# Down as a block product in seven products for all token pairs, with the sums of h made in gate and up

## The chip, the cores and the metric

The kernel runs on one core of a Trainium2 chip. A core has TensorE (matmuls, PE in the profile, its weight loads PEld), VectorE (DVE), ScalarE (ACT), GpSimd (POOL) and SyncE (SP), which here only issues transfers, and 16 DMA engines. The metric is the device time of one execution in microseconds (us); lower is better. Times of the kernel before: 2737.86 us, the median of three runs (2736.7 to 2738.58).

## What is computed

Two layers of an encoder with a width of 1024, for 1024 prompt tokens and 64 sample tokens, with the same weights. Each layer is a mixer (retention in layer 0, differential attention in layer 1, beside a memory attention), a product with w_o, a norm, the feed-forward part, and a norm. Cut to what the change touches:

```python
def _swiglu(x, w_gate, w_up, w_down):
    return (jax.nn.silu(x @ w_gate) * (x @ w_up)) @ w_down
...
        xp = _post_norm(xp, _swiglu(xp, w_gate[i], w_up[i], w_down[i]), ln2_g[i], ln2_b[i])
...
        xs = _post_norm(xs, _swiglu(xs, w_gate[i], w_up[i], w_down[i]), ln2_g[i], ln2_b[i])
```

`_post_norm(x, y, g, b)` is the layer norm of ALPHA * x + y. The inner width is 2816: 22 blocks of 128. h is the product of silu and up, and "down" is h @ w_down, 1088 x 2816 by 2816 x 1024.

## The kernel before

**Arithmetic.** Everything is fp32. A matmul takes operands that are split in a high and a low part (fp32r), and a product is three matmuls: high by high, high by low, low by high. The sample has its 64 high and 64 low rows in one operand of 128, so it needs two. Prompt tokens are eight tiles of 128 (0 to 7); tile 8 is the sample.

**Weights.** The class Weights plans all weights of the program in one list. A unit is loaded raw by SP's queue, split by ACT (high, L231) and by VectorE (low, L244; for units of 384 columns POOL), and put into a ring of 8192 words, eight slots of 128 x 512 pairs. It runs ahead of the matmuls: `mm` (L294) calls `pump` behind every matmul, and the plan spends a count of TensorE time on when a raw is loaded, a high and a low are made. Raws lie in two buffers of tag "raw" and in t4 buffers.

**Gate and up** (`gate_up`, L1109) is a block product in seven products (P1 to P7) over pairs of token tiles already. For each of the 22 blocks of the inner width, weights of w_gate and w_up come in sums that POOL makes (`combine` L411 to L413, `combine4` L416), and seven products of two groups of columns (288 and 256) follow each other. At the end of P3 and P4 VectorE makes h of a block, and SP's queue stores it to `hd[l, ff]` in DRAM (L1180, L1188). Its operands, the split transposed X, lie in XT.

**Down** (`down`, L1240) goes through the tiles in three groups, DOWN = ((8, 0, 1), (2, 3, 4), (5, 6, 7)). For each group, it streams w_down (22 blocks of 128 x 1024) and the columns of h (`load_h` L1228 to L1233), in steps of two blocks. ACT and VectorE split h (L323, L326). A tile's two halves of 512 columns accumulate over all 22 blocks in PSUM (tags S, pj and A, two buffers each). At a group's end `finish` (L1273) adds ALPHA * X, and the norm follows (bn_stats L576, the reciprocal root L568 on POOL, apply L590 and L591). In layer 0 the tile is then transposed on TensorE into XT for the next mixer (`to_xt`, `tr` L299), as one of the pending pieces that down and the mixer take up; in layer 1 it is stored as the output. X comes from `mid` in DRAM by POOL's queue (L1221), a group at a time.

**Order.** Each engine runs its instructions in the order in which the program issues them. A queue's transfers are issued in that order too, and one that waits for its buffer or its data holds those behind it.

## Time and profile before

| what | value |
|---|---|
| median of three runs | 2737.86 us |
| the profiled execution's own time | 2741.43 us |
| its span | 2739.6 us, granted clock 0.98 |
| TensorE busy | 2639.4 us (96%), 16394 matmuls |
| VectorE, ACT, POOL busy | 1635.5 (60%), 1119.2 (41%), 503.6 us (18%) |
| DMA | 278.91 MB, 102 GB/s on the mean |
| of that w_down | 132 loads of 512 KB, both layers |
| chain that ended last | PE 85%, DVE 8%, ACT 2%, DMA 2% |

The profile comes from one execution with the hardware profiler on. Its span is what the trace's clock runs over; the rest of its time, 1.8 us, lies around it. Busy times are shares of the whole span and a mean over stages with different limits, so that a stage is read from its own stretch. The chain that ended last goes back from the last instruction, at each step to what released it. A wait of one engine costs time only where this chain goes through it.

### The profile page before, as it was taken

The page shows a single profiled execution, that of the slowest core. Times are in us where ns is not written, and L with a number is a line of the kernel's source. Part 1 is how long each engine was busy: PE and PEld are TensorE (multiplying, and loading weights), DVE is VectorE, ACT ScalarE, POOL GpSimd, SP SyncE. Part 2 cuts the span into 40 slices and gives each one's busy share as a digit, 9 for nine tenths or more (in the row PEclk, how much of TensorE's full clock was granted, in tenths as well). Part 3 has the DMA queues.
Part 4 walks back from the last instruction along what each step waited for, and adds up shares of the span by engine and source line. Part 5 has one row for each costly group of instructions (what it writes and reads, how often), then busy time and mean ns, then how long its engine had stood idle before and what let it go on. Part 6 is the DMA issues. An engine that isn't in the chain of part 4 may idle for free.

```text
span 2739.6 us, 44532 instructions
## 1 busy us (share of the span) xinstructions
PE 2639.4 (96%) x16394; PEld 2378.4 (87%) x16394; DVE 1635.5 (60%) x3799; ACT 1119.2 (41%) x2690; POOL 503.6 (18%) x529
## 2 busy tenths in 40 slices
PE   8999999989999999999999999999899999999997
PEld 7988887779999999877899999987699999998776
DVE  5766667784444444556567777777854444445664
ACT  5522223243333333434355555663343333334332
POOL 0022222132222230011111111101232222210110
PEclk9999999999999999999999999999899999999999
DMA  7121111432222224655311111123322222247662
GB/s 234 43 59 50 51 51 62 142 122 74 77 71 76 83 79 152 215 200 171 128 57 48 49 46 45 45 74 123 127 73 85 73 78 71 77 138 225 213 207 78
DMA packets 296090, 278.91 MB, mean 102 GB/s; under 512 B 63104, under 2 KB 257152, under 8 KB 295872
## 3 DMA queue, kind: packets, MB, share of 16 engines
q1 hardware_dynamic: 289424, 252.74, 29.7%
q0 software_dynamic: 6448, 23.33, 2.4%
q8 instruction: 129, 2.11, 0.3%
q14 instruction: 89, 0.73, 0.1%
HBM read 224.36 MB, written 51.64 MB: 101 GB/s over the span
## 4 chain that ended last, share of the span: by engine, by line
PE 85%; DVE 8%; ACT 2%; DMA 2%; issue 1%; POOL 1%; SPq 0%; DVEq 0%; POOLq 0%; ACTq 0%
PE pspj L294 39%; PE psS L294 23%; PE psA L294 19%; PE psA L299 3%; ACT de L919 1%; DVE dmx L913 1%; DVE ring L244 1%; DVE st L576 1%; DVE X L1273 1%; PE psS L299 1%; POOL rstd L568 0%; ACT ring L231 0%; DVE XT L326 0%; DVE T L326 0%; DVE X L591 0%
## 5 line engine op out<-in xcount | busy, mean ns | idle before, releaser
L294 PE MATMUL pspj<-ring,XT 128*128 128x512 f32 (+2 forms) x3024 | 680.8, 369 | 11.2 <-DVE ring L244 7.5
L244 DVE TENSOR_TENSOR ring<-raw,ring 128x512 fp32r<-128x512 f32 x558 | 384.2, 702 | 428.8 <-ACT ring L231 428.1
L231 ACT ACTIVATE ring<-raw 128x512 fp32r<-128x512 f32 (+1 forms) x606 | 367.3, 620 | 590.3 <-PE pspj L294 382.6
L294 PEld LDWEIGHTS pspj<-ring,XT 128*128 128x128 f32 x3024 | 526.5, 192 | 72.8 <-DVE ring L244 10.2
L294 PE MATMUL psS<-ring,hT 128*128 128x512 f32 x1496 | 361.3, 395 | 10.8 <-ACT hT L323 7.7
L294 PEld LDWEIGHTS psS<-ring,hT 128*128 128x128 f32 x1496 | 276.8, 188 | 83.6 <-ACT hT L323 16.5
L294 PE MATMUL psA<-XT,ring 128*128 128x288 f32 x2112 | 316.4, 296 | 0.0
L294 PEld LDWEIGHTS psA<-XT,ring 128*128 128x128 f32 x2112 | 291.5, 189 | 0.0
L294 PE MATMUL pspj<-XT,ring 128*128 128x256 f32 (+1 forms) x2112 | 281.2, 282 | 1.0 <-DVE XT L326 1.0
L294 PEld LDWEIGHTS pspj<-XT,ring 128*128 128x128 f32 x2112 | 266.3, 190 | 1.6 <-DVE XT L326 1.4
L294 PE MATMUL psS<-T,ring 128*128 128x288 f32 (+1 forms) x1890 | 262.0, 290 | 1.1 <-DVE s L1185 1.1
L294 PEld LDWEIGHTS psS<-T,ring 128*128 128x128 f32 x1890 | 244.4, 189 | 6.4 <-DVE s L1185 1.6
L244 DVE TENSOR_TENSOR ring<-sum,ring 128x512 fp32r<-128x512 f32 x132 | 98.3, 745 | 180.8 <-ACT ring L231 180.7
L416 POOL TENSOR_TENSOR sum<-raw,sum 128x512 f32<-128x512 f32 x44 | 56.9, 1293 | 635.4 <-DVE ring L244 619.6
L568 POOL TENSOR_TENSOR rstd<-mv,mhalf 128x1 f32<-128x1 f32 (+1 forms) x36 | 67.5, 1874 | 533.6 <-DVE mv L579 533.6
L231 ACT ACTIVATE ring<-sum 128x512 fp32r<-128x512 f32 x132 | 83.4, 632 | 143.3 <-PE psS L294 83.7
L294 PE MATMUL pspj<-wx,XT 128*128 128x512 f32 x432 | 113.3, 399 | 0.0
L294 PE MATMUL psA<-T,ring 128*128 128x288 f32 x570 | 89.6, 309 | 17.3 <-ACT ring L231 13.7
L294 PE MATMUL pspj<-ring,hT 128*128 128x512 f32 x396 | 103.6, 389 | 0.0
L294 PE MATMUL psA<-ring,hT 128*128 128x512 f32 x396 | 102.3, 390 | 0.2
L919 ACT ACTIVATE de<-psS,dmx 128x512 f32<-128x512 f32 (+4 forms) x156 | 88.6, 584 | 28.7 <-DVE dmx L916 28.7
L294 PEld LDWEIGHTS psA<-T,ring 128*128 128x128 f32 x570 | 82.7, 200 | 19.1 <-ACT ring L231 15.2
(239 smaller groups left out, 3849.1 us busy)
## 6 DMA issues: line engine op xcount, KB each, us to landing
raw<-in_w_down_dram SPq DMA_DIRECT2D x132, 512.0 KB, 4.2
raw<-in_w_gate_dram SPq DMA_DIRECT2D x44, 512.0 KB, 3.7
raw<-in_w_up_dram SPq DMA_DIRECT2D x44, 512.0 KB, 4.0
hr<-hd SPq DMA_DIRECT2D x88, 192.0 KB, 4.2
raw<-in_w_o_dram SPq DMA_DIRECT2D x32, 512.0 KB, 3.5
hd<-s SPq DMA_DIRECT2D x88, 144.0 KB, 2.0
raw<-in_ret_w_in_dram SPq DMA_DIRECT2D x48, 256.0 KB, 3.6
hd<-s SPq DMA_DIRECT2D x88, 128.0 KB, 3.4
```

The source lines that it names most:

```text
L231: k.nc.scalar.activation(s[:, 0], src(), AF.Copy)
L244: e.tensor_tensor(s[:, 1], src(), s[:, 0].bitcast(F32), op=OP.subtract)
L294: self.nc.tensor.matmul(out, l, r, start=start, stop=stop, skip_group_check=chain)
L299: self.nc.tensor.transpose(out, in_, ident)
L416: self.nc.gpsimd.tensor_tensor(sums[ff][1], part(ff, 0, 1), sums[ff][1], op=OP.subtract)
L568: self.nc.gpsimd.tensor_tensor(r[:n], var, self.mhalf[:n], op=OP.pow)
L576: nc.vector.bn_stats(st[:n, e], X[:n, e * 512:(e + 1) * 512])
L913: nc.vector.reduce_max(mx[:n, 2 * j:2 * j + 2], sp[:n, :, :m], axis=AX.X)
L919: nc.scalar.activation(e[:n, c, 512 * j:512 * j + m], sp[:n, c, :m], AF.Exp, bias=mx[:n, 4 + c:5 + c], scale=0.125, accum_out=mx[:n, 6 + 2 ...
L1273: nc.vector.scalar_tensor_tensor(X[t][:n, cs], X[t][:n, cs], ALPHA, dp[e][:n], op0=OP.mult, op1=OP.add)
```

## The change

Down becomes a block product as gate and up is one. The 22 blocks of the inner width are taken as 11 pairs, the output's 1024 columns as two halves, and the tokens as four pairs of tiles, PAIRS = ((0, 2), (1, 3), (4, 6), (5, 7)). So each block product is two by two by two, and is done in seven products of sums of blocks instead of eight (order 1, 7, 6, 5, 4, 3, 2). A product goes over 11 f for all four token pairs at once, each pair in a PSUM bank of its own, and its result is added into X on VectorE (`take`), by the table TAKES. The products 1, 6 and 5 share banks. The sample keeps its eight blocks without sums: it uses the single blocks of w_down beside products 1, 5, 3 and 2.

The sums of h are made in gate and up: POOL makes one sum behind each even block and three behind each odd one (`operands`), in two stages at the ring's end. The ring of gate and up is shorter by that, seven slots. The seven operands of an f, 128 x 512 each, are stored to `ho[l, p, f]`, the sample's split rows to `hs`. In down, SP loads them back one by one and ACT and VectorE split them.

The sums of w_down are made in down, on POOL (`plan_down`, L581, L588, L599, L611), in a room that XT's memory becomes while down runs; XT is two tiles now for that reason. Blocks of w_down are loaded into this room by SP's queue, either to a place of their own ("own", L541) or by one of six spare buffers of two blocks (L223). The low parts of products 3 and 2 are made on POOL. The last five f of product 2 are done pair by pair. The norm of the second tiles (2, 3, 6, 7) stands in product 3, that of the sample and the first tiles at the end, and layer 1's mixer takes its memory items in that order. All X loads stand in product 1.

The diff, cut:

```diff
-DOWN = ((8, 0, 1), (2, 3, 4), (5, 6, 7))
+PAIRS = ((0, 2), (1, 3), (4, 6), (5, 7))
+FIRSTS = tuple(a for a, _ in PAIRS)
+SECONDS = tuple(b for _, b in PAIRS)
+ORDER = (1, 7, 6, 5, 4, 3, 2)
+NF = NFF // 2
+TAKES = {7: ((1, 0, True), (1, 1, True)), 1: ((0, 0, True),), 6: ((1, 0, False),),
+         5: ((0, 1, True), (1, 1, False)), 4: ((1, 0, False),), 3: ((0, 1, False),), 2: ((0, 0, False),)}
+TAIL = 5
...
+RING_GATE_UP = 7168
+SPARE = 6
...
+        if self.raws[j][1] == "spare" and not self.k.xt_free:
+            return False
+        if self.raws[j][1] == "own":
+            return self.k.xt_free and self.next_split >= self.late[j] - 4
...
-        e = self.k.nc.gpsimd if cols == 384 else self.k.nc.vector
...
+            W.ptr, W.limit = 0, RING_GATE_UP
             self.plan_gate_up(l)
+            W.ptr, W.limit = 0, RING_WORDS
+            self.plan_down(l)
...
+    def plan_down(self, l):
+        W = self.W
+        w = self.i["w_down"][l]
+        tt = self.nc.gpsimd.tensor_tensor
+        def block(f, odd, half):
+            return w[(2 * f + odd) * 128:(2 * f + odd + 1) * 128, half * 512:(half + 1) * 512]
+        def load(v, src):
+            return (lambda raw: raw[:, v, :], src)
+        def own(f):
+            return W.add_into(lambda: self.nc.sync.dma_start(self.b11(f), block(f, 0, 0)))
+        def pairs(odd, half):
+            out = {}
+            for f in range(0, NF, 2):
+                out[f] = [load(v, block(f + v, odd, half)) for v in range(min(2, NF - f))]
+            return out
+        def unit(p, f, raws, src, before=None, **kw):
+            u = self.u_d[l, p, f] = W.add_unit(512, raws, src, **kw)
+            if before:
+                W.before_split[u] = before
+            if p in (3, 2):
+                W.low_on_pool.add(u)
+            if p != 1 or f >= 4:
+                W.wait_xt.add(u)
+            return u
+        held = {}
+        todo = pairs(0, 0)
+        for f in range(NF):
+            if f < 4:
+                if f % 2 == 0:
+                    held[f] = W.add_raw(todo[f])
+                j = held[f - f % 2]
+                unit(1, f, [j], lambda j=j, f=f: W.raw[j][:, f % 2, :])
+            else:
+                held[f] = own(f)
+                unit(1, f, [held[f]], lambda f=f: self.b11(f))
+        for f in range(NF):
+            if f < 4:
+                held["own", f] = own(f)
+            j = W.add_raw([load(0, block(f, 0, 1)), load(1, block(f, 1, 1))], "spare")
+            def t3(j=j, f=f):
+                c = self.chain(f)
+                raw = W.raw[j]
+                tt(c, raw[:, 1], raw[:, 0], op=OP.subtract)
+                W.released.add(j)
+            unit(7, f, [j], lambda f=f: self.chain(f), t3)
+        for f in range(NF):
+            unit(6, f, [held["own", f] if f < 4 else held[f]], lambda f=f: self.chain(f),
+                 lambda f=f: tt(self.chain(f), self.chain(f), self.b11(f), op=OP.add))
+        todo = pairs(0, 1)
+        for f in range(NF):
+            if f % 2 == 0:
+                j = W.add_raw(todo[f], "spare")
+            def part(j=j, f=f):
+                return W.raw[j][:, f % 2, :]
+            unit(5, f, [j], lambda f=f: self.b11(f),
+                 lambda f=f, part=part: tt(self.b11(f), part(), self.b11(f), op=OP.subtract))
+            unit(0, f, [j], part)
+        todo = pairs(1, 0)
+        for f in range(NF):
+            if f % 2 == 0:
+                j = W.add_raw(todo[f], "spare")
+            def part(j=j, f=f):
+                return W.raw[j][:, f % 2, :]
+            unit(4, f, [j], lambda f=f: self.chain(f),
+                 lambda f=f, part=part: tt(self.chain(f), part(), self.chain(f), op=OP.subtract))
+        for p, odd, half in ((3, 1, 1), (2, 1, 0)):
+            todo = pairs(odd, half)
+            for f in range(NF):
+                if f % 2 == 0:
+                    j = W.add_raw(todo[f])
+                unit(p, f, [j], lambda j=j, f=f: W.raw[j][:, f % 2, :])
...
-            nc.sync.dma_start(self.hd[l, ff][:, c:c + w[g]], a)
         def P4(ff, g, last=True):
             product(ff, 4, g, False, last)
             a, b = tile(ff, "s1", g), tile(ff, "s2", g)
             nc.vector.tensor_tensor(b, s[ff, "c3", g][:, :w[g]], b, op=OP.add)
             nc.vector.tensor_tensor(a, a, b, op=OP.mult)
+            if last:
+                operands(ff)
+        later = deque()
+        def store(dst, src):
+            later.append([6, dst, src])
+        def flush(all=False):
+            for x in later:
+                x[0] -= 1
+            while later and (all or later[0][0] <= 0):
+                _, dst, src = later.popleft()
+                (nc.gpsimd if dst.dtype == F32R else nc.sync).dma_start(dst, src)
+        def stage(i):
+            return self.ring_end[:, 512 * i:512 * (i + 1)]
+        def operands(ff):
+            f, odd = ff // 2, ff % 2
+            a, b = s[ff, "s1"], s[ff, "s4"]
+            hs = self.sm([128, 128], "hn", 3, F32R)
...
+            a, b = a[:, 32:544], b[:, 32:544]
+            store(self.hs[l, odd, f // 4][:, f % 4, :], hs)
+            tt = nc.gpsimd.tensor_tensor
+            if not odd:
+                store(self.ho[l, 1, f], a)
+                tt(stage(0), a, b, op=OP.subtract)
+                store(self.ho[l, 7, f], stage(0))
+                return
+            a0, b0 = s[ff - 1, "s1"][:, 32:544], s[ff - 1, "s4"][:, 32:544]
+            tt(stage(1), b0, b, op=OP.add)
+            tt(b0, stage(1), a0, op=OP.subtract)
+            tt(a0, a, b0, op=OP.subtract)
+            for p, x in ((6, b0), (5, stage(1)), (4, b), (3, a0), (2, a)):
+                store(self.ho[l, p, f], x)
...
+            if ff == 1:
+                both = both[1:3] + both[:1] + both[3:]
...
+        for i in range(2):
+            self.load_h(l, i)
+        self.load_sample(l, 0, 0)
+    def load_h(self, l, i):
+        p, f = ORDER[i // NF], i % NF
+        raw = self.hraw[i] = self.s2([128, 512], name="hr")
+        self.nc.sync.dma_start(raw, self.ho[l, p, f])
...
+    def split_op(self, i):
+        raw = self.hraw.pop(i)
+        if i < 2:
+            x = self.t4([128, 2, 512], F32R, "hT")
+            if i == 0:
+                self.keep = x
+        else:
+            c = (i - 2) % 5
+            x = self.keep if c == 4 else self.hslots[c // 2][:, c % 2]
+        self.hop[i] = x
+        self.split_h(x[:, 0], raw)
+        self.split_l(x[:, 1], raw, x[:, 0])
...
+        self.room = [self.xtp.tile([128, NF + SPARE, 512], F32, name=f"room{e}_{self.cnt}", tag="xt", bufs=2) for e in range(2)]
+        self.xt_free = True
+        self.hslots = [self.h9([128, 2, 2, 512], F32R, "hT") for _ in range(2)]
...
+        def load_x(t):
+            X[t] = self.t4([128, D], name=f"X{t}")
+            nc.gpsimd.dma_start(X[t][:self.ncol(t)], self.mid[l, t])
...
+        def take(t, half, ps, first):
+            x = X[t][:, half * 512:(half + 1) * 512]
+            if first:
+                nc.vector.scalar_tensor_tensor(x, x, ALPHA, ps, op0=OP.mult, op1=OP.add)
+            else:
+                nc.vector.tensor_tensor(x, ps, x, op=OP.add)
...
+        def product(p, f, pair, out, start, stop):
+            s = W.get(self.u_d[l, p, f])
+            wh, wl = s[:, 0], s[:, 1]
+            h = self.hop[ORDER.index(p) * NF + f]
+            c = slice(128 * pair, 128 * pair + 128)
+            self.mm(out, h[:, 0, c], wh, start, False, 512, chain=True)
+            self.mm(out, h[:, 0, c], wl, False, False, 512, chain=True)
+            self.mm(out, h[:, 1, c], wh, False, stop, 512, chain=True)
...
+        for j, t in enumerate(FIRSTS + (8,) + SECONDS):
+            chore(1, 1 + j, lambda t=t: load_x(t))
...
+        for j, t in enumerate(SECONDS):
+            chore(3, 1 + 2 * j, lambda t=t: norm(t))
+        def banks(kind):
+            if kind == "S":
+                out = [self.ps([128, 2, 512], "S") for _ in range(2)]
+                return [out[0][:, 0], out[0][:, 1], out[1][:, 0], out[1][:, 1]]
+            return [self.ps([128, 512], t) for t in ("pj", "pj", "A", "A")]
+        V = None
+        ahead(0, 3, 2)
+        for k, p in enumerate(ORDER):
+            if p == 1:
+                V = banks("V")
+            dps = V if p in (1, 6, 5) else banks("S")
...
+            def end(pair):
+                for which, e, fresh in TAKES[p]:
+                    take(PAIRS[pair][which], e, dps[pair], fresh)
+            whole = NF if p != 2 else NF - TAIL
+            for f in range(whole):
+                i = k * NF + f
+                for fn in chores.get((p, f), ()):
+                    fn()
+                for pair in range(4):
+                    product(p, f, pair, dps[pair], f == 0 and p not in (6, 5), f == NF - 1 and p not in (1, 6))
+                    if f == NF - 1:
+                        end(pair)
+                    if pair == 1:
+                        ahead(i, 6, 3)
+                    elif pair == 3 and self.pending and p in (3, 2):
                         self.pending.popleft()()
...
+        ahead(7 * NF, 7 * NF, 7 * NF)
+        for f in range(whole, NF):
+            sample(f, odd, self.u_d[l, unit, f], sp)
+        take_sample(half, sp, first)
+        norm(8)
+        for pair in range(4):
+            for f in range(whole, NF):
+                product(2, f, pair, dps[pair], False, f == NF - 1)
+                if pair == 3:
+                    W.done(self.u_d[l, 2, f])
+            end(pair)
+            norm(FIRSTS[pair], FIRSTS[3])
+            if self.pending:
+                self.pending.popleft()()
+        self.xt_free = False
```

What stands on TensorE's queue early in down of layer 1. psS, pspj and psA are the PSUM tiles by tag, ring holds weights, hT split h of one block (before) or of one f of a product (after). Before:

```order
L294 MATMUL psS_25322<-ring,hT_25306 128x512 x3
L294 MATMUL pspj_25348<-ring,hT_25301 128x512 x2
L294 MATMUL pspj_25348<-ring,hT_25306 128x512 x3
L294 MATMUL psA_25349<-ring,hT_25301 128x512 x3
L294 MATMUL psA_25349<-ring,hT_25306 128x512 x3
```

After, one f of product 1 (hs is the sample's operand):

```order
L356 MATMUL pspj_25531<-ring,hT_25521 128x512 x3
L356 MATMUL pspj_25532<-ring,hT_25521 128x512 x3
L356 MATMUL psA_25533<-ring,hT_25521 128x512 x3
L356 MATMUL psA_25534<-ring,hT_25521 128x512 x3
L356 MATMUL psS_25535<-ring,hs_25221 128x512 x2
```

Before, a tile's two halves are finished for two blocks, six matmuls a bank, before the next tile; now a row of the block product has one weight for each of four banks, and the sample's two matmuls stand behind each f.

SP's queue some way into the same down, from where h of block 8 is loaded. hr is raw h, raw a raw weight. Before:

```order
L1228 DMA hr_25494<-hd_8_174 128x256
L1229 DMA hr_25494<-hd_8_174 128x32
L1230 DMA hr_25494<-hd_8_174 128x32
L1228 DMA hr_25498<-hd_9_175 128x256
L1229 DMA hr_25498<-hd_9_175 128x32
L1230 DMA hr_25498<-hd_9_175 128x32
L1228 DMA hr_25556<-hd_10_176 128x256
L186 DMA raw_25457<-in_w_down_dram 128x1024
```

After (room is XT's memory; L541 loads a block to its own place, L223 a spare pair, L1459 an operand):

```order
L223 DMA room_3066_25519<-in_w_down_dram 128x512 x2
L1459 DMA hr_25609<-ho_1_7_230 128x512
L541 DMA room_3066_25520<-in_w_down_dram 128x512
L223 DMA room_3066_25519<-in_w_down_dram 128x512 x2
L541 DMA room_3066_25520<-in_w_down_dram 128x512
L223 DMA room_3066_25519<-in_w_down_dram 128x512 x2
L223 DMA room_3066_25520<-in_w_down_dram 128x512 x6
L1459 DMA hr_25648<-ho_1_8_231 128x512
L223 DMA room_3066_25519<-in_w_down_dram 128x512 x2
L1459 DMA hr_25674<-ho_1_9_232 128x512
```

Before, every few loads of h there is one or two of w_down; after, five spare pairs and two single blocks stand between the operands of f = 7 and f = 8.

POOL's queue at the passage from gate and up to down in layer 1. Before, from the last block's sums (L1221 loads X):

```order
L413 TENSOR_TENSOR raw_24647<-raw_24612,raw_24647 128x512
L416 TENSOR_TENSOR sum_24766<-raw_24612,sum_24766 128x512
L1221 DMA X_3092_25287<-mid_8_143 64x1024
L1221 DMA X_3093_25289<-mid_0_135 128x1024
L1221 DMA X_3094_25291<-mid_1_136 128x1024
L1221 DMA X_3113_25434<-mid_2_137 128x1024
L1221 DMA X_3114_25436<-mid_3_138 128x1024
L1221 DMA X_3115_25438<-mid_4_139 128x1024
```

After (L1498 loads X, L1410 to L1416 are the sums of h, L1390 and L1464 the sample's store and load, L581 and L588 sums of w_down):

```order
L1498 DMA X_3089_25684<-mid_8_145 64x1024
L1498 DMA X_3091_25709<-mid_2_139 128x1024
L1414 TENSOR_TENSOR ring_20340<-s_3049_25200,s_3062_25429 128x512
L1498 DMA X_3094_25736<-mid_3_140 128x1024
L1415 TENSOR_TENSOR s_3049_25200<-ring_20340,s_3039_24998 128x512
L1390 DMA hs_1_2_311<-hn_25504 128x128
L1416 TENSOR_TENSOR s_3039_24998<-s_3054_25238,s_3049_25200 128x512
L1498 DMA X_3096_25761<-mid_6_143 128x1024
L1498 DMA X_3098_25786<-mid_7_144 128x1024
L1464 DMA hs_25593<-hs_0_1_307 128x512
L581 TENSOR_TENSOR room_3066_25519<-room_3066_25520 128x512
```

The nine X loads stand between the last sums of h now, all ahead of the first sum of w_down; before, six stood at the start and three further on, behind norms.

## Rows read from the trace of the kernel before

**Rows 1.** Table of stretches: PE, PEld, DVE, ACT, POOL busy; PEclk, DMA share, GB/s

```profile
598.00:1079.30 481.30, 471.00 (x3673) 467.14 (x3673) 216.88 (x393) 182.94 (x391) 124.10 (x91) 0.98 0.27 83
...
2458.50:2725.50 267.00, 264.39 (x1146) 212.09 (x1144) 150.96 (x274) 105.12 (x211) 23.78 (x13) 1.00 0.57 188
```

**Rows 2.** Matmuls in order of time: start, us, line, out<-in, count [idle before <-releaser]

```profile
1079.33 0.63 PE L294 MATMUL psS<-ring,hT 128*128 128x512 f32 x2
...
1363.31 3.05 PE L294 MATMUL pspj<-ring,XT 128*128 128x256 f32 x24
...
2458.53 0.63 PE L294 MATMUL psS<-ring,hT 128*128 128x512 f32 x2
...
2723.94 1.52 PE L294 MATMUL psA<-ring,hT 128*128 128x512 f32 x6
```

**Rows 3.** Chain that ended last, in order of time: start, us, what

```profile
2709.14 5.44 PE psS L294 x24
```

**Rows 4.** Waits of TensorE in layer 0's, then layer 1's down: total, times, longest

```profile
PE psS L294 <- ACT hT L323: 6.9, 9, 2.0
...
PE psS L294 <- DVE hT L326: 1.7, 2, 1.2
```

**Rows 5.** Transposes on TensorE, and its waits, at the start of layer 1's mixer

```profile
1367.32 0.66 PE L299 MATMUL pspj<-ident,X 128*128 128x128 f32 x4 [0.96 <-DVE X L591]
1367.81 0.60 PE L299 MATMUL psA<-ident,X 128*128 128x128 f32 x4
...
PE pspj L294 <- ACT qdup L615: 3.5, 3, 1.5
PE pspj L299 <- DVE X L591: 1.0, 1, 1.0
```

**Rows 6.** Table of stretches again, two with saturated DMA

```profile
1080.00:1084.00 4.00, 4.00 (x18) 3.32 (x18) 1.83 (x6) 1.15 (x4) 0.00 (x0) 1.00 1.04 387
...
15.00:20.00 5.00, 5.00 (x23) 4.13 (x22) 3.94 (x6) 3.17 (x5) 0.00 (x0) 1.00 1.04 404
```

**Rows 7.** Groups of instructions in layer 1's down: count, busy us, mean ns

```profile
L244 DVE TENSOR_TENSOR ring<-raw,ring 128x512 fp32r<-128x512 f32 x125 | 83.6, 689 | 95.8 <-ACT ring L231 95.7
L326 DVE TENSOR_TENSOR hT<-hr,hT 128x384 fp32r<-128x384 f32 x44 | 24.0, 549 | 0.4
L1273 DVE SCALAR_TENSOR_TENSOR X<-X,psS 128x512 f32<-128x512 f32 x10 | 6.6, 676 | 11.0 <-PE psS L294 11.0
...
L231 ACT ACTIVATE ring<-raw 128x512 fp32r<-128x512 f32 x125 | 76.7, 626 | 122.3 <-PE pspj L294 120.5
L323 ACT ACTIVATE hT<-hr 128x384 fp32r<-128x384 f32 x44 | 22.5, 516 | 11.7 <-DVE ring L244 5.9 <-DMA out_dram<-X 5.4
...
L244 POOL TENSOR_TENSOR ring<-raw,ring 128x384 fp32r<-128x384 f32 x48 | 53.5, 1141 | 59.1 <-PE pspj L294 47.3 <-ACT ring L231 11.4 <-issue 0.2
```

**Rows 8.** Matmuls in order of time at the start of layer 0's gate and up

```profile
604.26 0.85 PE L294 MATMUL psA<-T,ring 128*128 128x288 f32 x2 [6.14 <-ACT ring L231]
605.95 5.64 PE L294 MATMUL psA<-T,ring 128*128 128x288 f32 x22 [0.83 <-ACT ring L231]
```

**Rows 9.** POOL's, then VectorE's instructions in order of time, in gate and up

```profile
705.66 1.62 POOL L412 TENSOR_TENSOR sum<-sum,raw 128x512 f32<-128x512 f32 x1
707.25 1.28 POOL L413 TENSOR_TENSOR raw<-raw,raw 128x512 f32<-128x512 f32 x1
...
702.26 0.69 DVE L244 TENSOR_TENSOR ring<-sum,ring 128x512 fp32r<-128x512 f32 x1 [0.20 <-ACT ring L231]
705.29 0.84 DVE L244 TENSOR_TENSOR ring<-raw,ring 128x512 fp32r<-128x512 f32 x1 [2.33 <-ACT ring L231]
```

**Rows 10.** VectorE's last instructions of the kernel, in order of time

```profile
2734.24 1.41 DVE L591 SCALAR_TENSOR_TENSOR X<-X,rstd,gb 128x512 f32<-128x512 f32 x2
```

**Rows 11.** Matmuls in order of time, one product of gate and up in layer 0

```profile
1069.46 1.76 PE L294 MATMUL psA<-XT,ring 128*128 128x288 f32 x12
...
1072.48 1.76 PE L294 MATMUL psA<-XT,ring 128*128 128x288 f32 x12
```

325 lines of the change are left out of this document (180 added, 145 removed).

## The prediction

> **What bounds the kernel now.** First the table of stretches: from 598 to 1079 us (gate and up of layer 0) TensorE is busy 471 of 481 us, and in layer 1's down 264 of 267, at a granted clock of 0.98 and 1.00 [rows 1]. DMA is at 27% and 57%, VectorE under 60%. Then the list of matmuls in order of time, for the edges of the two downs: 1079.33 to 1363.31 us, 284.0 us, in layer 0, and from 2458.53 us to the end of the last six matmuls at 2725.46, 266.9 us, in layer 1 [rows 2]. Last the chain that ended last, which runs through TensorE alone until 2722.8: 24 matmuls of 512 columns in 5.44 us, 226.7 ns each [rows 3]. A down has 22 steps of 52 matmuls (sixteen halves of prompt tiles with three each, two of the sample with two each), 1144, which at that pace take 259.3 us. So layer 1's down loses 7.6 us to waits, and layer 0's loses 24.7, of which the tables of waits name 6.9 for operands that the group change left unsplit [rows 4], and six tile transposes take some 1.1 us each (eight in 1.1 us [rows 5]). Down is bound by the count of matmuls. A change of its count is worth 0.227 us a matmul as long as everything that feeds it keeps up, and that is the question here.
>
> **The change, part by part.**
>
> *Matmuls.* Seven products of 11 blocks, four token pairs, three matmuls each are 924; the sample keeps 4 x 11 units of two, 88. 1012 against 1144: 132 fewer a layer. 1012 x 0.2267 = 229.4 us a layer.
>
> *First operands and banks.* Product 1 starts when the last gate-and-up results have left the four banks that it takes. I charge 1.5 us a layer, the longer waits of the earlier starts being 1.2 to 2.0 us [rows 4].
>
> *The burst ahead of product 1.* This is the term I trust least. Before, loads went out a few at a time. Now nine X tiles (4.5 MB, by POOL's queue), eleven blocks of 256 KB (2.9 MB) and, by the SP order, seven spare pairs of half a megabyte (3.7 MB) stand ahead of the operand of f = 8, with three operands and gate and up's last stores (2 MB): 13 MB. The blocks and spares go where XT lay, so none can start before gate and up's last products. On SP the stores hold everything behind them until the last sums are made on POOL, some 4.5 us into the down; by then I count some 3.5 MB gone, 9.5 to go. The nearest saturated stretches moved 387 and 404 GB/s [rows 6]; at 385 it is 24.7 us, so the operand lands at about 30 us. Its step starts at 8 x 14 x 0.2267 = 25.4, and the split needs 1.9 before it (516 ns ACT and 549 ns VectorE for 384 columns, both a third more for 512, and the queue of the step before [rows 7]): needed at 23.5. Late by some 7 us, and a further 1 for a clock that falls in the gap: where TensorE had been idle for 6.1 us, the next 24 matmuls of 288 columns took 7.3 us [rows 8], against 3.1 at the warm pace (24 x 0.2267 x 288/512). I take 8 us a layer, bounds 0 (X served late, or the pairs spread) and 11.
>  The Trainium skill ("DMA: Bandwidth & Descriptors", Specifications) gives about 358 GB/s as the limit of one core at HBM. The two saturated rows are above it; by it the burst would take 26.5 us and the stall be 2 us longer in each layer.
>
> *Feeding the steady part.* In products 7, 6 and 4 a block f lasts 12 x 0.2267 = 2.72 us, in 1, 5, 3 and 2 (with a sample unit) 3.17. ACT splits a weight and an operand: 0.63 + 0.62 = 1.25 us. VectorE makes two lows, 2 x 0.69 = 1.38. POOL makes one weight sum, 1.28 to 1.62 [rows 9]. In product 5 there is a sample unit to split as well: ACT 1.9, VectorE 2.1, of 3.17. The lows that move to POOL (products 3 and 2) are 1141 ns for 384 columns, so some 1.52 for 512. None reaches the step [rows 7], so I cost all of this at nothing; TensorE covers it, and the margin is thin only where VectorE and POOL share. DMA over a whole down falls: 81 blocks of 256 KB instead of 66 of 512 KB, while operands rise from 12.2 to 20.2 MB, together 41.4 against 46.9 MB. "Once" is not what it does (once would be 11.5 MB), but nothing hangs on that.
>
> *Takes.* Eight at the end of product 7, two or one a pair elsewhere, 0.68 us each [rows 7], 5.2 us of VectorE at worst. Weights of up to six f and operands of up to four are ready by then, 10 us of matmuls: nothing.
>
> *Layer 0's transposes.* Seven tiles instead of six fall in down, 7.7 us. The last four norms come close together in the last five f, and the transposes wait for them: 2.1 us. In return the mixer of layer 1, whose first items found X unfinished (3.5 + 1.0 us of waits [rows 5]), starts with tiles that are done in product 3: I take 2.8 us off, with one transpose moved.
>
> *End.* The last pairs come 15 matmuls, 3.4 us, apart, and VectorE needs some 5.1 us for each (a take and two statistics of 0.7, the apply's two passes of 1.4, small ones [rows 10]), so the norms queue. Today VectorE ends at 2735.65, 10.2 us after TensorE; I get 11.6: +1.4. XT in two halves costs a few more small instructions in the prologue and behind w_o: +1.
>
> *Gate and up.* TensorE's count is unchanged: a product for both groups lasts 3.02 us (from 1069.46 to 1072.48 [rows 11]), seven of them 21.15 us a block. POOL is busy 124.1 us for 22 blocks, 5.6 a block [rows 1], and gains four sums every two blocks: 11.3 + 4 x 1.28 to 1.62 = 16.4 to 17.8 of 42.3 us. Ring slots fall from eight to seven, six products of lookahead, 18 us. By my count of the order, at 21.15 us a block, a block's buffers must be stored 24.7 us after its last product and are at 15.3, and POOL's weight sums have some 7 us in hand. I cost it at nothing; the cover is that slack of 7 to 9 us.
>
> *Sum.* Layer 0: 229.4 + 7.7 + 8 + 1.5 + 2.1 = 248.7, from 284.0: -35.3. Layer 1: 229.4 + 8 + 1.5 = 238.9, from 266.9: -28.0. Mixer -2.8, end +1.4, halves +1.0. Together -63.7, so 2741.4 of the profiled execution becomes 2677.7. That execution is 3.6 us above the median of the runs shown: 2674.
>
> **The rivals.**
>
> *No stall at all.* The SP order puts an operand between the blocks often enough. Against it: five of the spare pairs stand between the operands of f = 7 and f = 8. Then 16 us less: 2658.
>
> *VectorE and POOL exclude each other.* POOL sums and VectorE lows now run through all of down. A POOL sum beside VectorE took 1.62 us rather than 1.28, and the low beside it 0.84 rather than 0.69 [rows 9]. If they had to take turns, a step of products 7, 6 and 4 would take 1.38 + 1.28 to 1.62 = 2.66 to 3.00 of 2.72 us, one of product 5 3.35 to 3.69 of 3.17: 33 x 0.28 + 11 x 0.52 = 15 us a layer at most, 2 at least; I take 12. That gives 2698. For it: lookahead doesn't help against an average. Against: the overlap in that row cost 0.15 us a low, not a whole turn.
>  The Trainium skill ("SBUF — State Buffer", Who interferes with whom) has just this rule: a VectorE operation with two inputs in SBUF and a POOL operation that reads SBUF hold one port pair by turns. The rows' smaller stretch speaks for partial waits at most; 2698 would be its result here.
>
> *Gate and up gives it back (the slower side).* The odd block's three sums stand on POOL's queue behind a result that VectorE makes last, and the next block's weight sums stand behind them. If that holds up a weight sum, or a store holds a buffer, each block loses. The price is 44 blocks x the lateness beyond the slack; from 1.45 us a block (2.9 each odd block), 64 us are lost and the kernel is slower than 2738. At half of that it is 2706. For it: the tables show POOL's sums 1.3 to 1.6 us, so a chain of three is 4.5, and the slack is an estimate. Against: TensorE is 98% busy there today with POOL at a quarter [rows 1].
>
> *It doesn't cut the matmuls.* The order of the built kernel has them: 1012 a layer. No chance given.
>
> **How the numbers follow.** Forecast 0.50 (2674, own range 2668 to 2680); no stall 0.17 (2658); exclusion 0.20 (2698); gate and up late in part 0.08 (about 2685 to 2732); gate and up late in full 0.05, of which 0.02 ends within the bound and 0.03 beyond. About 0.2% of 2738, 5.5 us, is what a measurement can tell from no change. Faster 0.95, same 0.02, slower 0.03. The range takes in the first three with the bounds of their terms: 2658 less 6 (boundary and norms free: 1.5 + 1.5 + 2.1 and 1 of the halves), and the exclusion at its 15 us a layer, 2704, and 2 more for the stall's upper bound: 2652 to 2706.
>
> **What would show it.** Down's edges in the list of matmuls: 249 and 239 us. Right if a gap of 4 to 10 us stands at about 25 us into each down, ended by an operand's load or its split, with DMA share near 1 from 5 to 30 us. If the gap is missing: no stall. If the waits in products 7, 6, 4 and 5 are many small ones ended by VectorE's lows or POOL's sums, with both longer than 0.69 and 1.28 us: exclusion. If gate and up lasts more than 482 us, ended by POOL or by a store: the last rival. It would be wrong altogether if 24 matmuls in down took more than 5.44 us.

## The result, and the profile after

The changed kernel takes 2710.61 us (median of four runs, 2705.39 to 2711.54) against 2737.99 us: a ratio of 0.9897, interval 0.988 to 0.9914. A second set gave 0.9905 (0.9889 to 0.9922). It is faster, by 1.0%, but the forecast was 2.3% (2674 us), and the time lies above the range of 2652 to 2706. So the sign was right, and more than half of the gain didn't come.

The profiled execution has a span of 2708.7 us instead of 2739.6. Where the difference came from is read from TensorE's edges, matmuls in order of time as in [rows 2]: the first of gate and up and of down in layer 0, of the mixer and of gate and up in layer 1, of down there, and the last.

```profile
606.79 0.85 PE L356 MATMUL psA<-T,ring 128*128 128x288 f32 x2 [4.94 <-ACT ring L289]
...
1078.22 0.86 PE L356 MATMUL pspj<-ring,hT 128*128 128x512 f32 x3
...
1344.01 1.20 PE L356 MATMUL pspj<-ring,XT 128*128 128x256 f32 x8
...
1962.09 0.85 PE L356 MATMUL psA<-T,ring 128*128 128x288 f32 x2 [4.73 <-ACT ring L289]
...
2433.51 0.86 PE L356 MATMUL pspj<-ring,hT 128*128 128x512 f32 x3
...
2688.18 3.69 PE L356 MATMUL psS<-ring,hT 128*128 128x512 f32 x15 [1.19 <-DVE mv L771]
```

| stretch | before | after | gain | forecast |
|---|---|---|---|---|
| to gate and up, layer 0 | 604.3 | 606.8 | -2.5 | -0.5 |
| gate and up with down, layer 0 | 759.1 | 737.2 | 21.8 | 35.3 |
| mixer and w_o of layer 1 | 620.2 | 618.1 | 2.1 | 2.3 |
| gate and up with down, layer 1 | 742.0 | 729.8 | 12.2 | 28.0 |
| behind the last matmul | 14.1 | 16.8 | -2.7 | -1.4 |

Of the 33 us that are missing, 29 are in the two downs. Gate and up, where POOL now makes the sums of h, is not where they are. The table of stretches, gate and up first, then down, of each layer (columns as in [rows 1]):

```profile
606.00:1078.20 472.20, 467.30 (x3660) 463.40 (x3661) 234.79 (x426) 188.27 (x427) 194.79 (x156) 0.99 0.32 100
1078.20:1344.00 265.80, 247.92 (x1082) 200.31 (x1081) 186.57 (x248) 101.65 (x180) 121.10 (x96) 0.97 0.56 185
1962.00:2433.50 471.50, 467.23 (x3660) 463.34 (x3661) 234.03 (x425) 187.75 (x427) 194.01 (x155) 0.99 0.32 100
2433.50:2691.90 258.40, 242.08 (x1026) 194.70 (x1024) 179.85 (x237) 92.75 (x161) 116.83 (x91) 0.97 0.56 182
```

POOL's busy time in gate and up rises from 124 to 195 us, and TensorE needs 473 us with the twelve matmuls that stand behind down's first ones, against 475 before. In down, TensorE is busy 248 of 266 us and 242 of 258, where the forecast had 10 us of waits. The waits of TensorE in layer 0's down (columns as in [rows 4]):

```profile
PE psS L356 <- DMA hs<-hs: 6.9, 1, 6.9
PE pspj L356 <- ACT hT L385: 3.8, 1, 3.8
PE pspj L356 <- ACT g L1369: 1.6, 1, 1.6
PE psS L356 <- DVE s L1375: 1.3, 1, 1.3
PE psS L356 <- DVE X L1506: 1.2, 1, 1.2
```

(L356 is the matmul, L385 and L388 the two halves of an operand's split, L289 and L305 those of a weight's, as L294, L323, L326, L231 and L244 were.) Layer 1 has the same list: 6.9 for hs, 3.4 and 1.3 for hT. In order of time, at the end of product 1:

```profile
1109.57 0.61 PE L356 MATMUL psS<-ring,hs 128*128 128x512 f32 x2
1113.94 2.07 PE L356 MATMUL pspj<-ring,hT 128*128 128x512 f32 x4 [3.75 <-ACT hT L385]
1116.88 1.22 PE L356 MATMUL pspj<-ring,hT 128*128 128x512 f32 x2 [0.87 <-DVE hT L388]
...
1121.77 0.61 PE L356 MATMUL psA<-ring,hT 128*128 128x512 f32 x2
1129.33 1.22 PE L356 MATMUL psS<-ring,hs 128*128 128x512 f32 x2 [6.94 <-DMA hs<-hs]
```

The first gap, at f = 8, is the one that the prediction describes. Twenty matmuls, 4.5 us of work, take from 1110.0 to 1122.2 at a clock that falls to 0.5: 7.7 us are lost in layer 0 and 7.8 in layer 1, where 8 were put. The second one is not in the prediction. TensorE waits for hs, the sample's operand of f = 8, and loses 9.5 us a layer with the clock.

What POOL does there, in order of time (L581 is a sum of weights for product 7, L588 for product 6, L1464 the sample's load):

```profile
1101.77 1.28 POOL L581 TENSOR_TENSOR room<-room 128x512 f32<-128x512 f32 x1 [12.01 <-DMA room<-in_w_down_dram]
1104.51 1.29 POOL L588 TENSOR_TENSOR room<-room,room 128x512 f32<-128x512 f32 x1 [1.47 <-DVE ring L305]
1105.76 1.74 POOL L581 TENSOR_TENSOR room<-room 128x512 f32<-128x512 f32 x1
...
1119.62 3.41 POOL L581 TENSOR_TENSOR room<-room 128x512 f32<-128x512 f32 x2
1122.99 1.26 POOL L588 TENSOR_TENSOR room<-room,room 128x512 f32<-128x512 f32 x1
1124.19 0.57 POOL L1464 DMA_DIRECT2D hs<-hs  x1
```

The sample's third load is issued at 1124.19, behind a row of weight sums that begins at 1101.77, 23 us into the down, because the first waits 12 us for a block. It lands 5 us later. Between two sums for product 7, which is next, stands one for product 6, which isn't needed for 40 us and more. The text ahead of the prediction says that each engine goes in the order of the program; there all sums for product 7 come first, so the built queue isn't in that order.

The first gap has another cause than these sums. On SP's queue the operand of f = 8 stands behind the spare pairs; from 1094 us to its issue, each wait of that queue ends with a transfer that lands, and none with a POOL sum. The operand lands 5.4 us after its issue, at 1113.14, and ACT splits it 0.13 us after that, although a split that waited for a sum stands ahead of it (SP's issue and its time to landing, then ACT):

```profile
1107.79 0.33 SPq L1459 DMA_DIRECT2D hr<-ho  x1
...
DMA to landing us min/median/max: 5.4/5.4/5.4
...
1112.73 0.63 ACT L289 ACTIVATE ring<-room 128x512 fp32r<-128x512 f32 x1 [0.59 <-POOL room L581]
1113.27 0.61 ACT L385 ACTIVATE hT<-hr 128x512 fp32r<-128x512 f32 x1
```

VectorE and POOL, some 35 us further on, in product 7, again in order of time (L599 is a sum for product 5):

```profile
1149.62 1.78 DVE L388 TENSOR_TENSOR hT<-hr,hT 128x512 fp32r<-128x512 f32 x1
1151.33 1.77 DVE L305 TENSOR_TENSOR ring<-room,ring 128x512 fp32r<-128x512 f32 x1
...
1149.12 1.74 POOL L588 TENSOR_TENSOR room<-room,room 128x512 f32<-128x512 f32 x1
1150.81 3.44 POOL L599 TENSOR_TENSOR room<-room,room 128x512 f32<-128x512 f32 x2
```

The busy time of that stretch (columns as in [rows 1]):

```profile
1145.00:1160.00 15.00, 14.13 (x62) 10.98 (x61) 15.00 (x10) 6.84 (x13) 15.00 (x10) 1.00 0.25 70
```

Two engines are busy 15.00 of 15 us, with ten instructions each. A VectorE low, 0.69 us by itself, lasts 1.7 to 1.8, and so does a POOL sum that takes 1.28 by itself: one of each every 1.70 us.

### The profile page after: what moved, and what is told of

The parts are those of the page before. It is cut to its first block, busy times and chain, and to the rows that moved or that the text cites. A ratio compares the mean times of both kernels' runs of the same rounds, so it can differ in the third digit from the quotient of the medians.

```text
span 2708.7 us, 44487 instructions
## 1 busy us (share of the span) xinstructions
PE 2584.6 (95%) x16130; PEld 2335.9 (86%) x16130; DVE 1726.9 (64%) x3821; ACT 1109.4 (41%) x2702; POOL 837.8 (31%) x809
## 4 chain that ended last, share of the span: by engine, by line
PE 80%; DVE 8%; issue 4%; DMA 3%; POOL 2%; ACT 2%; SPq 0%; POOLq 0%; DVEq 0%; ACTq 0%
PE pspj L356 39%; PE psA L356 19%; PE psS L356 19%; PE psA L361 3%; DMA room<-in_w_down_dram 2%; ACT de L1111 1%; DVE dmx L1105 1%; PE psS L361 1%; DVE XT L388 1%; DVE X L782 1%; DVE X L783 1%; DVE ring L305 1%; DVE hT L388 1%; POOL room L581 0%; DVE en L1060 0%
## 5 line engine op out<-in xcount | busy, mean ns | idle before, releaser
L356 PE MATMUL pspj<-ring,XT 128*128 128x512 f32 (+2 forms) x3024 | 681.7, 370 | 11.6 <-DVE X L1265 5.6
L356 PEld LDWEIGHTS pspj<-ring,XT 128*128 128x128 f32 x3024 | 527.6, 193 | 73.9 <-DVE ring L305 7.2
L305 DVE TENSOR_TENSOR ring<-raw,ring 128x512 fp32r<-128x512 f32 x302 | 215.3, 723 | 225.1 <-ACT ring L289 222.7
L289 ACT ACTIVATE ring<-raw 128x512 fp32r<-128x512 f32 (+1 forms) x394 | 236.8, 614 | 242.0 <-PE pspj L356 64.4
L356 PE MATMUL psA<-XT,ring 128*128 128x288 f32 x2112 | 315.8, 295 | 1.6 <-ACT s L1363 1.6
L356 PEld LDWEIGHTS psA<-XT,ring 128*128 128x128 f32 x2112 | 289.9, 188 | 2.2 <-ACT s L1363 2.0
L356 PE MATMUL pspj<-XT,ring 128*128 128x256 f32 (+1 forms) x2112 | 281.0, 282 | 2.5 <-DVE XT L388 1.2
L356 PEld LDWEIGHTS pspj<-XT,ring 128*128 128x128 f32 x2112 | 266.1, 190 | 3.7 <-DVE XT L388 1.7
L356 PE MATMUL psS<-T,ring 128*128 128x288 f32 (+1 forms) x1890 | 263.5, 291 | 2.5 <-DVE s L1375 2.5
L356 PE MATMUL psS<-ring,hT 128*128 128x512 f32 x1056 | 251.1, 392 | 5.3 <-DVE X L1506 2.3
L356 PEld LDWEIGHTS psS<-T,ring 128*128 128x128 f32 x1890 | 245.7, 190 | 8.0 <-DVE s L1375 3.1
L356 PEld LDWEIGHTS psS<-ring,hT 128*128 128x128 f32 x1056 | 196.4, 188 | 52.8 <-DVE X L1506 3.6
L388 DVE TENSOR_TENSOR hT<-hr,hT 128x512 fp32r<-128x512 f32 x154 | 152.3, 996 | 109.5 <-ACT hT L385 97.2
L305 DVE TENSOR_TENSOR ring<-sum,ring 128x512 fp32r<-128x512 f32 x132 | 99.9, 756 | 150.5 <-ACT ring L289 150.5
L385 ACT ACTIVATE hT<-hr 128x512 fp32r<-128x512 f32 x154 | 96.2, 630 | 209.6 <-PE psS L356 120.8
L305 POOL TENSOR_TENSOR ring<-raw,ring 128x384 fp32r<-128x384 f32 (+1 forms) x92 | 113.6, 1250 | 123.2 <-ACT ring L289 70.8
L760 POOL TENSOR_TENSOR rstd<-dmx,mhalf 128x1 f32<-128x1 f32 (+1 forms) x54 | 30.4, 563 | 360.9 <-DVE dmx L1163 295.9
L305 DVE TENSOR_TENSOR ring<-room,ring 128x512 fp32r<-128x512 f32 x124 | 98.6, 815 | 49.2 <-ACT ring L289 48.8
L289 ACT ACTIVATE ring<-sum 128x512 fp32r<-128x512 f32 x132 | 83.3, 631 | 86.4 <-PE pspj L356 78.7
L356 PE MATMUL pspj<-ring,hT 128*128 128x512 f32 x396 | 107.5, 406 | 11.4 <-ACT hT L385 7.2
L356 PE MATMUL pspj<-wx,XT 128*128 128x512 f32 x432 | 113.3, 399 | 0.0
L289 ACT ACTIVATE ring<-room 128x512 fp32r<-128x512 f32 x124 | 74.8, 621 | 85.2 <-PE psS L356 50.9
```

The costliest lines, as they stand in the source:

```text
L289: k.nc.scalar.activation(s[:, 0], v, AF.Copy)
L305: e.tensor_tensor(s[:, 1], v, s[:, 0].bitcast(F32), op=OP.subtract)
L356: self.nc.tensor.matmul(out, l, r, start=start, stop=stop, skip_group_check=chain)
L385: self.nc.scalar.activation(h, src, AF.Copy)
L388: self.nc.vector.tensor_tensor(l, src, h.bitcast(F32), op=OP.subtract)
L760: self.nc.gpsimd.tensor_tensor(r[:n], var, self.mhalf[:n], op=OP.pow)
```

## The experiments

The kernel before was run beside each set; its medians were 2743.8, 2742.3, 2738.6 and 2739.8 us, so the kernels are compared by their ratio to it. The changed kernel is at 0.9897 and 0.9905.

**The sample's loads earlier.**

```diff
-        chore(1, 2, lambda: self.load_sample(l, 0, 1))
-        chore(1, 6, lambda: self.load_sample(l, 0, 2))
+        chore(1, 0, lambda: self.load_sample(l, 0, 1))
+        chore(1, 1, lambda: self.load_sample(l, 0, 2))
```

> Only the second and third loads of the sample's split h are asked for two and five f earlier, so that on POOL's queue they stand ahead of the first weight sum instead of behind twelve. Queue theory (the 6.9 us wait of TensorE in each down is the load's place behind the sums): both waits go, with the clock that falls in them, 9.5 us a layer; the wait for the operand of f = 8 stays at 4 to 5 us: 2710.6 - 19 = 2692 us. Bandwidth rival (DMA is at full share there, so something else of the same burst is late instead): a wait of 4 us or more for an operand or a weight comes at f = 9 to product 7's start, and the time stays above 2703.

Measured: 2703.84 us, ratio 0.9858 (0.9839 to 0.9877). The wait for hs is gone from the list, so its place behind the sums was its cause. But by the ratios only 11 to 13 of the 19 us were won: the wait for VectorE at the end of product 7 grew from 1.2 to 3.4 us, and 0.9 for the sample's take is new.

```profile
PE psS L356 <- DVE X L1506: 3.4, 1, 3.4
PE pspj L356 <- ACT hT L385: 2.7, 1, 2.7
```

**Operands nine f ahead as well.** The same edit, and

```diff
-                        ahead(i, 6, 3)
+                        ahead(i, 9, 3)
```

> As the run with the sample's loads early, and operands are loaded nine f ahead instead of six, so that on SP's queue the operand of f = 8 stands ahead of all spare pairs. Queue theory for the operand (it was late because it stood behind spare pairs, the seventh of which waits for POOL's first sum to release its buffer): its wait of 4 to 5 us goes too, 7 us a layer with the clock: 2678 us. Bandwidth theory, that of the prediction (9.5 MB had to pass before it): the operand comes no earlier than its share of the burst or the spares come late instead, and product 7's start waits: 2687 to 2692.

Measured: 2705.99 us, 0.9867 (0.9846 to 0.9889). The wait at f = 8 is gone too: product 1 runs through. So the operand was late by its place on SP's queue, and not by bandwidth alone: DMA moved 380 GB/s here as well (1095 to 1110 us). And the time stayed: product 7's start now waits 3.6 us for VectorE's lows and 4.6 for its take.

```profile
PE psS L356 <- DVE X L1516: 4.6, 1, 4.6
PE psS L356 <- DVE hT L388: 3.6, 2, 2.0
```

**X of the second tiles in product 7.** The sample's loads early, and

```diff
-            chore(1, 1 + j, lambda t=t: load_x(t))
+            chore(*((1, 1 + j) if j < 5 else (7, 2 * j - 9)), lambda t=t: load_x(t))
...
-            nc.gpsimd.dma_start(X[t][:self.ncol(t)], self.mid[l, t])
+            q = nc.sync if t in SECONDS else nc.gpsimd
+            q.dma_start(X[t][:self.ncol(t)], self.mid[l, t])
```

> As the run with the sample's loads early, and the X of the second tiles (2, 3, 6, 7; 2.1 MB) is loaded in product 7 by SP's queue instead of at the start of down by POOL's. Bandwidth theory: 2.1 MB less in the burst is 5.4 us at 385 GB/s, so the operand of f = 8 is in time: 2678 us. Queue theory: it still stands behind the seventh spare pair, which waits for POOL's first sum; that sum waits for its spare pair's transfer, which may land 3 us earlier: wait 2 to 4 us, 2684 to 2691.

Measured: 2699.22 us, 0.9837 (0.9818 to 0.9857). Its interval overlaps that of the first run. At f = 8 it waits 2.5 us instead of 4.1, which is near what the queue theory said; with 2.1 MB less in the burst the wait didn't go, as the bandwidth theory had it.

**All three.**

> All three at once: sample's loads early, operands nine f ahead, X of the second tiles in product 7. Both theories: no wait over 1 us from f = 8 to product 7's start, 2676 us. If the time stays over 2685, a third cause holds product 1 or 7.

Measured: 2699.7 us, 0.9844 (0.9829 to 0.9858): the case for a third cause. Nothing waits until product 7, and there 3.5 us stand for VectorE's lows and 5.5 for the take, 2.3 at its end.

**Product 6's sums behind all of product 7's.** The sample's loads early, operands nine ahead, and

```diff
-                tt(c, raw[:, 1], raw[:, 0], op=OP.subtract)
+                self.sum7 = tt(c, raw[:, 1], raw[:, 0], op=OP.subtract).ins
...
+        def sum6(f):
+            with self.tc.issue_after(self.sum7):
+                tt(self.chain(f), self.chain(f), self.b11(f), op=OP.add)
...
-                 lambda f=f: tt(self.chain(f), self.chain(f), self.b11(f), op=OP.add))
+                 lambda f=f: sum6(f))
```

> As the run with the sample's loads early and operands nine f ahead (2706), and on POOL's queue the sums for product 6 stand behind all eleven for product 7 instead of one between each two. That run waits 2.0 + 1.6 + 4.6 us at the start of product 7 in layer 0. Queue theory (product 7's sums are late because product 6's stand between them and wait for VectorE's low): these waits go, 8 us a layer with the clock: 2690. Exclusion theory (POOL and VectorE take turns, VectorE's operations last 1.5 to 3 us there instead of 0.69): POOL has half the work there, VectorE's times fall only in part: 2698. Bandwidth theory (the spare pairs land late): no change, 2703 to 2706.

Measured: 2702.92 us, 0.9867 (0.9847 to 0.9887), the same as without. At product 7's start 3.1 us are left of 8.2, and at its end the wait for the takes is 9.1, as the waits of TensorE show. The order only moved the place.

```profile
PE psS L356 <- DVE X L1510: 9.1, 1, 9.1
PE psS L356 <- DVE X L1520: 3.1, 1, 3.1
```

VectorE and POOL are both full from 1130 to 1160, and TensorE gets 10.8 of 15 us; the second half of that as a row of the table of stretches:

```profile
1145.00:1160.00 15.00, 10.82 (x48) 8.50 (x46) 15.00 (x10) 4.30 (x8) 15.00 (x10) 1.00 0.48 156
```

**The sums of w_down on VectorE.** One word of the changed kernel, in `plan_down`:

```diff
-        tt = self.nc.gpsimd.tensor_tensor
+        tt = self.nc.vector.tensor_tensor
```

> The changed kernel with nothing altered but the engine of the weight sums in down: VectorE instead of POOL. If the sums on POOL are the root of all three waits (the sample's load behind them on POOL's queue, the operand of f = 8 behind weight splits on ACT that wait for them, VectorE's slow lows): 2710.6 - 25 = 2685. If they are the root of the sample's wait alone: 2700. If VectorE's queue is held by sums that wait for loads: 2710 or more.

Measured: 2684.79 us, 0.9798 (0.9777 to 0.9819): 1.0 to 1.1% below the changed kernel, as much as the whole change had brought. VectorE has 44 more operations in each down, yet is busy 13.85 of 15 us where it was full, with 23 instructions instead of ten, and TensorE doesn't wait there (table of stretches):

```profile
1145.00:1160.00 15.00, 15.00 (x67) 12.14 (x66) 13.85 (x23) 5.45 (x10) 0.00 (x0) 1.00 0.52 176
```

The wait for hs is gone, since nothing stands ahead of the load, and so are those around product 7; at f = 8 the one for the operand is left, at 5.0 us, so that POOL's sums were not its cause. The groups of an operand's and a weight's lows in layer 0's down, in the changed kernel:

```profile
L388 DVE TENSOR_TENSOR hT<-hr,hT 128x512 fp32r<-128x512 f32 x75 | 73.7, 989 | 53.1 <-ACT hT L385 45.9 <-PE pspj L356 5.0 <-PE psS L356 2.0
L305 DVE TENSOR_TENSOR ring<-room,ring 128x512 fp32r<-128x512 f32 x62 | 49.3, 815 | 25.6 <-ACT ring L289 25.4
```

And here, with 0.81 and 0.69 us for one instead of 0.99 and 0.82:

```profile
L388 DVE TENSOR_TENSOR hT<-hr,hT 128x512 fp32r<-128x512 f32 x75 | 60.3, 807 | 47.9 <-ACT hT L385 37.9 <-PE pspj L356 5.0 <-PE psS L356 4.8
L305 DVE TENSOR_TENSOR ring<-room,ring 128x512 fp32r<-128x512 f32 x62 | 41.3, 685 | 8.6 <-ACT ring L289 8.4
```

**The same with loads early and operands nine ahead.**

> As the run with the sample's loads early and operands nine f ahead (2706), and all sums of w_down are made on VectorE instead of POOL. Exclusion theory: with no POOL sum beside it a low or a sum takes 0.69 us, three a block f are 2.1 of 2.72 us, and the waits at product 7's start fall to 2 us a layer: 2690. Queue theory: product 6's sums still stand between product 7's, but at half the time: 2695. Bandwidth theory: 2703 to 2706. Against it: sums now stand on VectorE's queue ahead of other work and can hold it up while they wait for a load.

Measured: 2684.24 us, 0.9796 (0.9773 to 0.9819). Against the run with those two edits and POOL's sums (0.9867) this is the exchange of the engine again. The two edits themselves bring nothing measurable here: the wait at f = 8 went, and 2.9 us for the sample's take and 1.7 at the passage stand instead.

**POOL's work without anybody who waits for it.** The run just told, and POOL copies each sum's size of work into a tile that nothing reads:

```diff
+        def tt(out, a, b, op):
+            self.nc.vector.tensor_tensor(out, a, b, op=op)
+            self.nc.gpsimd.tensor_tensor(self.nowhere, out, self.nowhere, op=OP.subtract)
```

> As the run with the sums on VectorE, the sample's loads early and operands nine f ahead (2684), and behind each of these sums POOL makes an operation of the same form and size that reads the sum and writes a tile that nothing else reads. Nobody waits for these results, so what they cost is what POOL's work beside VectorE costs. If the two take turns, VectorE's sums, lows and operand lows last 1.3 us and more instead of 0.69 while POOL is busy, and product 7's start or end waits 4 to 8 us a layer: 2692 to 2700. If POOL's sums hurt only because weights and loads wait for them: 2684.

Measured: 2755.45 us, 1.0062 (1.0044 to 1.008): 71 us more than the same kernel without these 88 operations, far over what was expected. So POOL's work costs by its presence. (Their one consequence for others, that a sum's place may not be overwritten before POOL has read it, shows in no row of VectorE's waits.) VectorE's and POOL's instructions in layer 0's down, in order of time:

```profile
1127.54 1.77 DVE L388 TENSOR_TENSOR hT<-hr,hT 128x512 fp32r<-128x512 f32 x1
1129.23 0.68 DVE L534 TENSOR_TENSOR room<-room 128x512 f32<-128x512 f32 x1
1129.83 0.68 DVE L305 TENSOR_TENSOR ring<-room,ring 128x512 fp32r<-128x512 f32 x1
1130.43 1.27 DVE L1510 SCALAR_TENSOR_TENSOR X<-X,pspj 128x512 f32<-128x512 f32 x2
...
1127.16 1.60 POOL L535 TENSOR_TENSOR nowhere<-room,nowhere 128x512 f32<-128x512 f32 x1 [1.90 <-DVE room L534]
1130.05 1.58 POOL L535 TENSOR_TENSOR nowhere<-room,nowhere 128x512 f32<-128x512 f32 x1 [1.29 <-DVE room L534]
```

And the groups of the weights' lows and of POOL's copies in that down:

```profile
L305 DVE TENSOR_TENSOR ring<-room,ring 128x512 fp32r<-128x512 f32 x62 | 64.7, 1061 | 7.0 <-ACT ring L289 7.0
L535 POOL TENSOR_TENSOR nowhere<-room,nowhere 128x512 f32<-128x512 f32 x44 | 69.4, 1578 | 89.5 <-DVE room L534 88.3
```

The low at 1127.54 begins while a POOL operation runs, which ends at 1128.76; it takes 1.77 us and ends 0.55 behind that. The one at 1129.83 is under way when the next POOL operation starts; it takes 0.68, and POOL's takes 1.58 instead of 1.28. The mean of the weights' lows is 1.06, POOL's 1.58. Of the two takes from 1130.43, which have one input in PSUM, each takes 0.64, beside a POOL operation that runs until 1131.63.

**The passage.** The run with the sums on VectorE, and product 1's splits that read the room are held behind gate and up's last silu on ACT and its last product of h on VectorE (on ACT, and likewise for the lows):

```diff
-        k.nc.scalar.activation(s[:, 0], v, AF.Copy)
+        if u in self.hold:
+            with k.tc.issue_after(k.last_act):
+                k.nc.scalar.activation(s[:, 0], v, AF.Copy)
```

> As the run with the sums on VectorE and nothing else (2685), and ACT's and VectorE's first seven weight splits of product 1 that read the new room are held behind gate and up's last silu and last product of h. Theory: TensorE's 1.3 to 2.5 us of waits at the passage, which come from the silu standing behind a split that waits for its load, shrink by half, with the clock 2 us a layer: 2681. Rival: these waits are the time that the last products' own chain takes, and the splits were in nobody's way: 2685.

Measured: 2684.67 us, 0.9802 (0.9788 to 0.9817): no difference in the time. In its trace both waits at layer 0's passage are gone (so the splits were in the way), and 1.1 us for hs has come at f = 0 instead; whether 1 or 2 us are won can't be told by these runs.

**POOL's lows of products 3 and 2 on VectorE too.** `if p in (3, 2): W.low_on_pool.add(u)` is left out.

> As the run with the sums on VectorE (2685), and the lows of products 3 and 2 on VectorE as well, so that POOL makes nothing in down but the norm's roots. If POOL's lows cost nothing, as the prediction has it: 2685. If they slow VectorE's norms (apply passes of 1.45 to 1.55 us there rather than 1.27) and so the first mixer items: 2682. If VectorE becomes the bound of product 3 (two lows 1.4 us, four norms of 5 us in 35 us): 2687 or more.

Measured: 2686.97 us, 0.9812 (0.9798 to 0.9827), the same within the intervals. The norm's passes fell from 1.45 and 1.55 to 1.36 and 1.29 us and operand lows to 0.72, and nobody waits for them there.

**All that helped.** Sums on VectorE, sample's loads early, operands nine ahead, X of the second tiles in product 7, splits held.

> Sums on VectorE, sample's loads early, operands nine f ahead, X of the second tiles in product 7 by SP's queue, and the splits held at the passage. If the waits left over in the run with the sums on VectorE (5.0 and 3.7 us for the operand of f = 8, 1.3 and 2.6 at the passages) are all that separates it from the forecast: 2674. If, as in the run with the sums on VectorE and the loads early, a wait of 2 to 3 us for the sample's take comes in their place: 2679.

Measured: 2678.22 us (2670.06 to 2680.29), 0.9775 (0.9757 to 0.9793): faster than both kernels, 2.2% under the one before. What is left in each down is 3.6 and 4.2 us for the sample's take, whose PSUM bank product 7 needs.

The changed kernel itself was in that set once more:

> The changed kernel as it is, on the same chip as the three beside it, for comparison: 0.9897 of the kernel before, as measured first.

Measured: 2711.85 us, 0.9905.

## Why the prediction was wrong

**Matmuls: right.** 1012 a down, 24 of them still in 5.44 us where nothing waits (a step of 12 is 2.72 us in product 6). With the sums on VectorE the stretches of gate and up with down last 722.1 and 717.5 us, a gain of 37.0 and 24.5, where the forecast for the changed kernel had 35.3 and 28.0. The sum's structure holds; what failed is what it took to be free.

**The step that failed** is "Feeding the steady part", where POOL's sums beside VectorE's lows were costed at nothing, and with it the dismissal of the rival that priced them. Two things in it were wrong. First, the row: the low of 0.84 us in [rows 9] began at 705.29, when the POOL sum ahead of the one shown was 0.3 us from its end, and the sum shown began beside it and took 1.62. The POOL sum ahead, in order of time, is this:

```profile
704.28 1.29 POOL L411 TENSOR_TENSOR sum<-raw 128x512 f32<-128x512 f32 x1
```

I read 0.15 us as the price of an overlap. It was the rest of a turn. In down the price is a whole turn, 1.0 us a low (1.7 for 0.69). Second, the count: I set one POOL sum against two lows an f. From 1101.8 to 1162.8 us, in which TensorE goes through some 15 f, POOL makes 33 sums, eleven each for products 7, 6 and 5, and VectorE 28 lows. So two POOL operations stand against two lows, 3.4 us of turns against TensorE's 2.72. By the exchange of the engine all this is worth 26 us. In the changed kernel's own waits most of it shows as the sample's load behind these sums, 9.5 us a layer, and only some 2 us a layer as waits for VectorE around product 7; with that load out of the way, VectorE's waits grow.

The Trainium skill ("SBUF — State Buffer", Who interferes with whom) states the rule that the prediction held to be too strong: a VectorE operation with two inputs in SBUF contends with a POOL operation that reads SBUF, for a port pair that one of them locks, and one with at most one SBUF input, outside the two-port modes, doesn't. The rows agree in both halves: 1.77 against 0.68 us, and 0.64 for the take from PSUM.

**The rival by exclusion** had the mechanism, and 2698. The measured time is 13 us above it; the rival counted only VectorE's rate, and POOL's sums reached TensorE in one more way. The sample's load stood behind them on POOL's queue (9.5 us a layer; the prediction names POOL's queue for X and not for hs).

**The burst: right in cause, and in size partly by luck.** 7.7 and 7.8 us were lost at f = 8, with DMA at full share, against 8 forecast, and the operand did stand behind the spare pairs. But the gap came 32 us into the down instead of 25, and the operand landed at 35 instead of 30; the two errors nearly cancel. The wait was 4.6 us where 7 were put, and the slower clock behind it cost 3 where 1 was put. (The loads counted there add up to 13.9 MB, not 13.) Operands that were asked for earlier came in time at 380 GB/s, so their place on SP's queue decides, and the burst alone doesn't. Taken away by itself the gap brought nothing, because VectorE and POOL were next.

**Passage: too small.** 5.0 and 3.9 us of TensorE's time instead of 1.5 (in layer 0 9.1 us for 4.15 of work, at a granted clock of 0.81). ACT's silu stood behind a split that waited for a block; with the splits held those waits went, but the time didn't change.

**End and halves: somewhat small.** 2.7 instead of 1.4, and 2.5 ahead of gate and up instead of 0.5. **Gate and up: right**, no time was lost there; the slower rival fell with it.

**Mixer: right in number, not in mechanism.** It gained 2.1 against 2.3, but the waits at its start, which the term was to shorten from 4.5 us [rows 5], became 5.4 (waits of TensorE, 1344 to 1381 us):

```profile
PE pspj L361 <- DVE X L783: 3.0, 1, 3.0
PE pspj L356 <- DVE ring L305: 2.4, 1, 2.4
```

The gain lies further on, and the mixer's stretch differs by as much between kernels that leave it alone (615.0 to 621.6 us).

How the 26 us divide is known in part. With the sample's loads and the operands early on both sides, the exchange of the engine is still worth 19 us (0.9867 against 0.9796; gate and up with down are 10.9 and 9.9 us shorter), near the 12 a layer that the rival had. So most of it isn't the place of those two loads. What stays open is how much of the 19 us is the turns and how much POOL's slower pace for a sum (1.28 against 0.69 us). The copies on POOL show that its work beside VectorE can cost more than that without anybody waiting for it, but they aren't the same work. And the time to the first matmul of gate and up in layer 0 lies between 605.0 and 609.7 us in these kernels, although none of them alters what is ahead of it; why is open, and it is of the size of the differences between the runs with the sums on VectorE.

## What to carry to other kernels

Before a sum is put on POOL because POOL is idle, count VectorE's operations with two SBUF inputs in the same stretch and let them take turns; VectorE's 0.69 us for the sum itself was the cheaper place, although VectorE was the busier engine. A row with a small overlap can show the rest of a turn and not its price: lay both engines' start and end times beside each other before a cost is taken from it. A load on a computing engine's queue stands behind that engine's work, as the sample's did for 9.5 us a layer. And where several engines feed the one that bounds, a wait taken away only brings time if the next feeder keeps up, so look for the engine pair that is busy the whole stretch, not for the wait with the largest number.
